# A feed-forward down-projection whose last product of each block is made in two halves

## The chip, the cores and the metric

The kernel runs on one core of a Trainium2 chip. The metric is the time of one execution on the device in microseconds (us). The core has four engines that matter here: TensorE (PE in the profile; PEld are its weight loads), VectorE (DVE), ScalarE (ACT) and GpSimd (POOL). DMA queues bring the weights from the chip's memory; SP issues these DMAs.

## The reference

One decoder layer: 256 tokens of width 1024 in float32. A normalised input goes through one combined projection into two token mixers, a recurrent one (RWKV-7) and a block-sparse attention (MoBA). Both are projected back, gated, merged, sent through an output projection and added to the input. The second half is the feed-forward part, which is where the change lies:

```python
def conv_ffn(h, w_up, conv_w, conv_b, w_down):
    u = h @ w_up
    a, b = u[..., :D_FF], u[..., D_FF:]
    a = lax.conv_general_dilated(
        a, conv_w.reshape(CONV_WIDTH, 1, D_FF), window_strides=(1,),
        padding=[(CONV_WIDTH - 1, 0)], dimension_numbers=('NWC', 'WIO', 'NWC'),
        feature_group_count=D_FF) + conv_b
    return (jax.nn.gelu(a, approximate=False) * b) @ w_down
```

with D_FF = 2816; the layer's output is x + conv_ffn(h2), where h2 is the normalised x.

## The kernel before

**Products in halves.** TensorE is used with operands rounded to a shorter float format (float32r). To keep the accuracy, each operand is split into a high and a low part (ACT rounds the high part, DVE makes the low part as the remainder), and a product of two matrices is made as three: high x high, low x high and high x low. All three accumulate into the same PSUM tile. So whatever is computed by `pe.matmul` in the kernel comes in groups of three lines: 346, 348, 351 in the helper `wst` (weights are the stationary operand and 256 tokens the moving one), 367, 368, 371 in `xst` (tokens stationary, up to 512 weight columns moving), and 1464, 1466, 1468 in the down-projection.

**Weights.** A queue lists all weight blocks of the layer in the order of their use. A block has 128 partitions by 1024 floats, 512 KB. A DMA on SP's queue brings it into a `raw` buffer (4 of them), `split_hi` (line 299, nearly always ACT) writes `whi` (4 buffers) and `split_lo` (line 310, DVE) writes `wlo` (3 buffers). The function `weights()` hands out the next pair and at once issues the split of a later block and the load of another one behind that. A `whi` or `wlo` buffer is written again only once the products that read it are done, so the splits wait on products.

**The feed-forward part.** The 2816 hidden columns are worked off in 11 blocks of 256, j = 0 to 10. In each block:

- `up()` makes 256 columns of the first half of the up-projection: four weight blocks, 48 products of 256 columns (8 pieces of the contraction x 2 groups of 128 hidden columns x 3). The stationary operand is `whi` or `wlo`, the moving one is `hx`, the normalised tokens in their high and low parts. DVE and ACT scale it, convolve it and apply GELU.
- `up(atp)` makes the matching 256 columns of the second half, 48 products again. DVE multiplies the two, and the result is split into high and low (`hb`).
- `down(j - 1)` makes the down-projection of the block before. It runs one block late, so that `hb` is ready when TensorE gets there.

`down` takes two weight blocks (i = 0, 1), one for each 128 hidden columns. For each it goes over four quarters of the output, f = 0 to 3: token half t by output half hf. Each quarter is an accumulator `fin[f]` of 128 tokens by 512 columns, a whole PSUM bank, held through all 11 blocks. Each quarter gets three products of 512 columns with `hb` as the stationary operand and `whi` or `wlo` as the moving one. That makes 2 x 4 x 3 = 24 products of 512 in a row. The next instruction on TensorE is the next block's `up()` with its 48 + 48 products of 256 columns.

`down` is called for j = 0 to 9. The block j = 10 is written out behind the loop (lines 1522 to 1524): its first three quarters in 18 products of 512 columns, the fourth in 12 products of 256 columns, six of them into a free accumulator, so that the last results leave in smaller pieces. For j = 9 the row of 24 is therefore followed by another 18 of 512.

**Order.** The feed-forward part is written out in program order; no planner chooses it. Each engine works off its own instructions in that order, and semaphores connect them. Every `pe.matmul` becomes two instructions of TensorE, a weight load for the stationary operand and the product itself.

Of the kernel before, what the change touches and what calls it, by code (L numbers as in the profile page):

```python
# [37 lines left out]
def body(tc, x, positions, norm1_g, w_in, rwkv_mu, w_decay_up, decay_bias, w_aaa_up,  # L38
# [3 lines left out]
    act, dve, pool, pe = nc.scalar, nc.vector, nc.gpsimd, nc.tensor  # L42
    ctx = ExitStack()
    with ctx:
# [12 lines left out]
        def b4(name, shape=(128, 4, 256), dt=F32):  # L57
            return sb.tile(list(shape), dt, name=name, tag="b4", bufs=NB4)
# [14 lines left out]
        def chp(name="ch"):  # L73
            return ps.tile([128, 512], F32, name=name, tag="ch", bufs=3)

        def atp(name="at"):
            return ps.tile([128, 512], F32, name=name, tag="at", bufs=2)
# [243 lines left out]
        def weights(n=1):  # L321

            w = ready.pop(0)
            taken[0] += 1
            for _ in range(n):
                with tc.issue_after(fence[0]) if taken[0] < 6 else nullcontext():
                    split_lo()
                    split_hi()
            return w
# [1093 lines left out]
        for i, (c0, c1) in enumerate(zip(WCUT, WCUT[1:])):  # L1423
            cs = slice(c0, c1)
# [31 lines left out]
        def down(j, hb):  # L1456
            for i in range(2):
                wh, wl = weights()
                st = j == 0 and i == 0
                for f in range(4):  # L1460
                    t, hf = divmod(f, 2)
                    ts = slice(t * 128, t * 128 + 128)
                    cs = slice(hf * 512, hf * 512 + 512)
                    pe.matmul(fin[f], hb[:, 0, i, ts], wh[:, 0, cs], start=st, stop=False,  # L1464
                              skip_group_check=f == 3)
                    pe.matmul(fin[f], hb[:, 1, i, ts], wh[:, 0, cs], start=False, stop=False,  # L1466
                              skip_group_check=f == 3)
                    pe.matmul(fin[f], hb[:, 0, i, ts], wl[:, 0, cs], start=False, stop=False,  # L1468
                              skip_group_check=f == 3)

        prev = []
        for j in range(11):
            hb = b4("hb", (128, 2, 2, 256), F32R)
            if j == 0:
# [3 lines left out]
                fin = [chp("f0"), chp("f1"), chp("f2"), atp("f3")]  # L1478
# [24 lines left out]
            if len(prev) == 2:  # L1503
                down(*prev.pop(0))
        of = out.rearrange("b s d -> (b s) d")
        j, hb = prev.pop(0)
# [6 lines left out]
        for f, is_ in ((0, (0,)), (1, (0,)), (0, (1,)), (2, (0,)), (1, (1,)), (2, (1,)), (3, (0, 1)), (4, (0, 1))):  # L1513
            t, hf = divmod(min(f, 3), 2)
            ts = slice(t * 128, t * 128 + 128)
            c0, n = ((0, 512), (0, 256), (256, 256))[max(f - 2, 0)]
            fs = last if f == 4 else fin[f][:, c0:c0 + n]
            cs = slice(hf * 512 + c0, hf * 512 + c0 + n)
            kw = dict(skip_group_check=True) if f == 3 else {}
            for i in is_:  # L1520
                wh, wl = ws[i]
# [32 lines left out]
```

## Time and profile before

| what | value |
|---|---|
| three timed runs | 402.75, 402.79, 403.62 us, median 402.79 |
| the profiled execution's own time | 402.01 us |
| its span, from the first instruction to the last | 400.2 us |
| PE busy | 394.3 us, 99% of the span |
| PEld busy | 365.9 us, 91% |
| DVE busy | 301.9 us, 75% |
| ACT busy | 237.3 us, 59% |
| the ten calls of `down` in the profile | 238.2 to 391.4 us, 80 products on each of the three lines |

A product's duration in the profile isn't what it costs. Products are pipelined and overlap: one with 256 columns is shown with about 277 ns, one with 512 with about 390 ns. What counts for the time is the distance between the starts of two neighbouring products. The timeline of PE shows these starts with two decimals of a microsecond, so distances are best read over many products at once.

Two more conventions of the rows: `f<-whi,hb` names the tile that is written and the tiles that are read (f is any of the four accumulators `fin`), and in a row of the groups the number behind the bar is the busy time, the mean duration in ns, and then the idle time of the engine just before these instructions. In a table by stretches each row has the stretch, its length, then PE, PEld, DVE, ACT and POOL with busy time and count, the granted clock of TensorE, the share of the DMA engines and GB/s.

### The profile page before, as it was taken

To read this page: it belongs to the slowest core of one execution; us is meant where nothing else is said; L and a number is where in the kernel's file an instruction comes from. 1 tells how busy PE (TensorE), PEld (TensorE's weight loads), DVE (VectorE), ACT (ScalarE), POOL (GpSimd) and SP (SyncE) were. 2 spreads that over 40 slices of the span, in tenths; PEclk is the share of its full clock that TensorE was granted. 3 is DMA by queue.
4 is the path that set the end of the run, shared out by engine and by line. 5 is a ranking of instruction groups with operands and counts; after the bars stand their busy time and mean duration, and the time that the engine had idled before them with its cause. 6 is when DMAs were issued, how large, how long until landed. Compare 5 with 4: busy or idle time off the path is not lost.

```text
span 400.2 us, 9024 instructions
## 1 busy us (share of the span) xinstructions
PE 394.3 (99%) x3633; PEld 365.9 (91%) x3633; DVE 301.9 (75%) x508; ACT 237.3 (59%) x411; POOL 49.5 (12%) x87
## 2 busy tenths in 40 slices
PE   8999999999999999999999999999999999999996
PEld 6899999898999989999888999999999999999995
DVE  4989989899868989688875885765757667576583
ACT  5899477494747686635554874554545546455350
POOL 8888000010600021120000000000000000000000
PEclk9999999999999999999999999999999999999999
DMA  8943397554694333555661765666665565665612
GB/s 255 323 147 86 86 305 219 139 153 124 145 292 128 108 98 128 201 162 185 199 195 56 261 206 184 196 189 195 191 208 186 185 208 168 204 211 163 208 52 105
DMA packets 60589, 70.58 MB, mean 176 GB/s; under 512 B 7377, under 2 KB 51287, under 8 KB 60548
## 3 DMA queue, kind: packets, MB, share of 16 engines
q1 hardware_dynamic: 58116, 69.17, 56.1%
q10 hardware_dynamic: 1632, 0.59, 0.6%
q8 instruction: 28, 0.46, 0.5%
q0 software_dynamic: 800, 0.26, 0.4%
q14 instruction: 13, 0.11, 0.1%
HBM read 68.56 MB, written 1.44 MB: 175 GB/s over the span
## 4 chain that ended last, share of the span: by engine, by line
PE 85%; POOL 4%; DMA 4%; DVE 3%; ACT 1%; issue 1%; SPq 0%; POOLq 0%
PE acc L346 11%; PE acc L351 11%; PE acc L348 11%; PE at L351 5%; PE at L346 5%; PE at L348 5%; PE f L1468 5%; PE f L1466 5%; PE f L1464 5%; PE acc L367 4%; PE acc L371 4%; PE acc L368 4%; DMA posi<-in_positions_dram 2%; PE acc L1322 2%; PE pq L1323 1%; DMA p<-in_aaa_bias_dram 1%
## 5 line engine op out<-in xcount | busy, mean ns | idle before, releaser
L299 ACT CAST whi<-raw 128x1024 fp32r<-128x1024 f32 (+1 forms) x122 | 124.5, 1025 | 111.3 <-PE acc L348 44.0
L310 DVE TENSOR_TENSOR wlo<-raw,whi 128x1024 fp32r<-128x1024 f32 (+1 forms) x122 | 144.6, 1188 | 37.7 <-PE f L1468 14.4
L346 PE MATMUL acc<-hx,whi 128*128 128x256 f32 x400 | 99.4, 284 | 0.0
L348 PE MATMUL acc<-hx,whi 128*128 128x256 f32 x400 | 97.1, 279 | 0.0
L346 PEld LDWEIGHTS acc<-hx,whi 128*128 128x128 f32 x400 | 75.4, 188 | 2.4 <-issue 0.8
L348 PEld LDWEIGHTS acc<-hx,whi 128*128 128x128 f32 x400 | 75.4, 188 | 0.4
L351 PE MATMUL acc<-hx,wlo 128*128 128x256 f32 x400 | 62.3, 278 | 0.2 <-DVE rs L1440 0.2
L351 PEld LDWEIGHTS acc<-hx,wlo 128*128 128x128 f32 x400 | 53.2, 188 | 0.4 <-DVE wlo L310 0.4
L346 PE MATMUL at<-hx,whi 128*128 128x256 f32 x176 | 42.4, 278 | 0.0
L348 PE MATMUL at<-hx,whi 128*128 128x256 f32 x176 | 42.3, 277 | 0.0
L348 PEld LDWEIGHTS at<-hx,whi 128*128 128x128 f32 x176 | 33.1, 188 | 0.0
L346 PEld LDWEIGHTS at<-hx,whi 128*128 128x128 f32 x176 | 33.1, 188 | 0.0
L1468 PE MATMUL f<-wlo,hb 128*128 128x512 f32 x80 | 31.6, 395 | 0.0
L1466 PE MATMUL f<-whi,hb 128*128 128x512 f32 x80 | 31.4, 393 | 0.0
L1464 PE MATMUL f<-whi,hb 128*128 128x512 f32 x80 | 31.2, 390 | 0.0
L351 PE MATMUL at<-hx,wlo 128*128 128x256 f32 x176 | 27.3, 277 | 0.0
L351 PEld LDWEIGHTS at<-hx,wlo 128*128 128x128 f32 x176 | 23.3, 188 | 0.0
L1466 PEld LDWEIGHTS f<-whi,hb 128*128 128x128 f32 x80 | 15.0, 188 | 3.1
L1468 PEld LDWEIGHTS f<-wlo,hb 128*128 128x128 f32 x80 | 15.1, 189 | 3.0
L1464 PEld LDWEIGHTS f<-whi,hb 128*128 128x128 f32 x80 | 15.0, 188 | 2.9
L1482 DVE TENSOR_TENSOR an<-acc,rsb 128x512 f32<-128x512 f32 x11 | 7.6, 692 | 13.1 <-PE acc L351 12.9
L1499 DVE TENSOR_TENSOR cv<-cv,at 128x256 f32<-128x256 f32 x22 | 8.3, 417 | 10.2 <-PE at L351 9.9
(359 smaller groups left out, 696.2 us busy)
## 6 DMA issues: line engine op xcount, KB each, us to landing
raw<-in_w_ffn_up_dram SPq DMA_DIRECT2D x44, 512.0 KB, 3.6
raw<-in_w_in_dram SPq DMA_DIRECT2D x33, 512.0 KB, 4.7
raw<-in_w_ffn_down_dram SPq DMA_DIRECT2D x22, 512.0 KB, 3.4
raw<-in_w_out_dram SPq DMA_DIRECT2D x8, 512.0 KB, 4.2
raw<-in_w_in_dram SPq DMA_DIRECT2D x8, 272.0 KB, 2.9
early<-in_w_in_dram SPq DMA_DIRECT2D x2, 1024.0 KB, 8.1
raw<-in_w_branch_b_dram SPq DMA_DIRECT2D x4, 512.0 KB, 3.5
raw<-in_w_branch_a_dram SPq DMA_DIRECT2D x4, 512.0 KB, 3.4
```

The source lines that it names most:

```text
L299: act.copy(wide(hi, k, c), spread(raw, k, c))
L310: eng.tensor_tensor(wide(lo, k, c), spread(raw, k, c), wide(hi, k, c).bitcast(F32), op=OP.subtract)
L346: pe.matmul(om, wh[:, k, ms], xh[:, k0 + k], start=k0 + k + m == 0, stop=False, skip_group_check=True)
L348: pe.matmul(om, wh[:, k, ms], xl[:, k0 + k], start=False, stop=False, skip_group_check=True)
L351: pe.matmul(om, wl[:, k, ms], xh[:, k0 + k], start=False, stop=k0 + k == nk - 1 and m == n - 1, skip_group_check=True)
L367: pe.matmul(ps_[t], xh[:, K, ts], wh[:, k], start=K == 0, stop=False)
L368: pe.matmul(ps_[t], xl[:, K, ts], wh[:, k], start=False, stop=False)
L371: pe.matmul(ps_[t], xh[:, K, ts], wl[:, k], start=False, stop=K == nk - 1)
L1464: pe.matmul(fin[f], hb[:, 0, i, ts], wh[:, 0, cs], start=st, stop=False, skip_group_check=f == 3)
L1466: pe.matmul(fin[f], hb[:, 1, i, ts], wh[:, 0, cs], start=False, stop=False, skip_group_check=f == 3)
L1468: pe.matmul(fin[f], hb[:, 0, i, ts], wl[:, 0, cs], start=False, stop=False, skip_group_check=f == 3)
L1499: dve.tensor_tensor(cv, cv, pb[:, m], op=OP.mult)
```

## The change

The third product of the last quarter (f = 3) of the second weight block (i = 1) is no longer one product of 512 columns. It is made as two of 256 columns, on the left and the right half of the same accumulator, with the same stationary operand. All other products of `down` stay as they are, and so does the order. A call of `down` has then 23 products of 512 columns in a row and two of 256 behind them.

```diff
                     pe.matmul(fin[f], hb[:, 1, i, ts], wh[:, 0, cs], start=False, stop=False,
                               skip_group_check=f == 3)
-                    pe.matmul(fin[f], hb[:, 0, i, ts], wl[:, 0, cs], start=False, stop=False,
-                              skip_group_check=f == 3)
+
+                    for c in ((0, 512),) if f < 3 or i == 0 else ((0, 256), (256, 512)):
+                        pe.matmul(fin[f][:, c[0]:c[1]], hb[:, 0, i, ts],
+                                  wl[:, 0, hf * 512 + c[0]:hf * 512 + c[1]], start=False, stop=False,
+                                  skip_group_check=f == 3)
```

## The prediction

> **What bounds the kernel now.** The page comes first: span, engine totals and the chain that ended last.
>
> ```profile
> span 400.2 us, 9024 instructions
> PE 394.3 (99%) x3633; PEld 365.9 (91%) x3633; DVE 301.9 (75%) x508; ACT 237.3 (59%) x411; POOL 49.5 (12%) x87
> ...
> PE 85%; POOL 4%; DMA 4%; DVE 3%; ACT 1%; issue 1%; SPq 0%; POOLq 0%
> ```
>
> The chain runs on TensorE (PE) for 85% of the span, and there is one weight load for each product: 3633 of both. The second view is the table by stretches, cut at the feed-forward part: one down-projection, the two up-projections of the next block, one down-projection, and then all nine later blocks together.
>
> ```profile
> 238.20:243.80 5.60, 5.60 (x26) 4.56 (x25) 3.78 (x6) 2.55 (x5) 0.00 (x0) 1.00 0.62 199
> 243.80:249.30 5.50, 5.50 (x50) 5.49 (x49) 2.45 (x2) 2.32 (x3) 0.00 (x0) 1.00 0.56 183
> 249.30:254.70 5.40, 5.40 (x50) 5.40 (x49) 4.54 (x7) 3.83 (x7) 0.00 (x0) 1.00 0.65 193
> 254.70:260.20 5.50, 5.50 (x26) 4.53 (x25) 3.79 (x6) 2.56 (x5) 0.00 (x0) 1.00 0.67 205
> 238.30:385.80 147.50, 147.50 (x1081) 138.61 (x1079) 97.02 (x135) 78.14 (x109) 0.00 (x0) 1.00 0.60 190
> ```
>
> The second column is PE: busy in every microsecond from 238.3 to 385.8, at a granted clock of 1.00. DVE is busy for 97.0 and ACT for 78.1 of those 147.5 us, so neither can be what ends last here. Nothing in this part waits; its time is the number of products times the distance from one start to the next (the pitch). The third view, the groups by line and shape in the same stretch, has no idle time before any of the three lines that the change touches:
>
> ```profile
> L1468 PE MATMUL f<-wlo,hb 128*128 128x512 f32 x72 | 28.4, 395 | 0.0
> L1466 PE MATMUL f<-whi,hb 128*128 128x512 f32 x72 | 28.3, 393 | 0.0
> L1464 PE MATMUL f<-whi,hb 128*128 128x512 f32 x72 | 28.1, 390 | 0.0
> ```
>
> The 390 to 395 ns in these rows are durations of overlapping products. What a product costs is the pitch, which has to come from the timeline of PE. Here is one down-projection with its neighbours: first its first product, then its last two, then the first products of the next up-projection, then the starts of the up-projection after it and of the next down-projection.
>
> ```profile
> 271.11 0.39 PE L1464 MATMUL f<-whi,hb 128*128 128x512 f32 x1
> ...
> 276.14 0.39 PE L1466 MATMUL f<-whi,hb 128*128 128x512 f32 x1
> 276.37 0.39 PE L1468 MATMUL f<-wlo,hb 128*128 128x512 f32 x1
> 276.61 0.28 PE L346 MATMUL acc<-hx,whi 128*128 128x256 f32 x1
> 276.72 0.28 PE L348 MATMUL acc<-hx,whi 128*128 128x256 f32 x1
> 276.84 0.28 PE L346 MATMUL acc<-hx,whi 128*128 128x256 f32 x1
> 276.96 0.28 PE L348 MATMUL acc<-hx,whi 128*128 128x256 f32 x1
> 277.08 0.28 PE L346 MATMUL acc<-hx,whi 128*128 128x256 f32 x1
> 277.20 0.28 PE L348 MATMUL acc<-hx,whi 128*128 128x256 f32 x1
> ...
> 282.07 0.28 PE L346 MATMUL at<-hx,whi 128*128 128x256 f32 x1
> 287.51 0.39 PE L1464 MATMUL f<-whi,hb 128*128 128x512 f32 x1
> ```
>
> Three pitches follow. (a) 24 products of 512 columns take 276.61 - 271.11 = 5.50 us: 0.229 each. (b) The 48 products of 256 in the second up-projection take 287.51 - 282.07 = 5.44 us: 0.1133 each. (c) The 48 of the first take 282.07 - 276.61 = 5.46, and the excess lies at their beginning: the first five take 277.20 - 276.61 = 0.59 where five at (b) take 0.567. So a change from down to up costs about 0.025 us. The whole of what follows agrees with these three:
>
> ```profile
> 243.81 0.28 PE L346 MATMUL acc<-hx,whi 128*128 128x256 f32 x1
> ...
> 385.91 0.39 PE L1464 MATMUL f<-whi,hb 128*128 128x512 f32 x1
> ```
>
> Between these rows lie nine blocks of up-projections, 9 x 96 products, and eight down-projections, 8 x 24. 864 x 0.1133 + 192 x 0.229 + 9 x 0.025 = 142.1 us, and 385.91 - 243.81 is 142.10. So all nine changes from down to up end at the pace (b).
>
> There is a second pace, and the argument on the risk rests on it. Just before, the same up-projection code ran slower, and so did the first down-projection:
>
> ```profile
> 222.54 0.41 PE L1445 MATMUL prs<-ident,rx 128*128 128x128 f32 x2
> 222.79 0.24 PE L1446 MATMUL prs<-ident,p 88*128 88x88 f32 x1
> 222.82 0.36 PE L346 MATMUL at<-hx,whi 128*128 128x256 f32 x1
> ...
> 232.56 0.28 PE L346 MATMUL at<-hx,whi 128*128 128x256 f32 x1
> ...
> 238.21 0.40 PE L1464 MATMUL f<-whi,hb 128*128 128x512 f32 x1
> ```
>
> 48 products from 232.56 to 238.21 take 5.65 us: 0.1177 each, 4.4 ns over (b). 24 products from 238.21 to 243.81 take 5.60: 0.2333, 4.2 ns over (a). The slow pace sets in after three small transposes cut into the stream, and it lasts, with the clock at 1.00 and PE without idle, until the change from down to up at 243.81, after which (b) holds. The trace doesn't say what the pace is. It says that an interruption can set it, that it then stays, and that a change of shape can end it.
>
> **The change part by part.** It touches the third product (line 1468) of the fourth quarter (f = 3) of the second weight block (i = 1), in each of the ten calls of `down` (j = 0 to 9; the block j = 10 is written out behind the loop and stays). It removes 10 products of 512 columns and adds 20 of 256, with 10 more weight loads since each product has its own. Order, operands, waits and DMAs stay.
>
> **The pair itself.** The nearest row is in the tail, where products with the same kinds of operands, on the same accumulator, go from 512 to 256 columns:
>
> ```profile
> 395.29 0.40 PE L1524 MATMUL f<-wlo,hb 128*128 128x512 f32 x1
> 395.53 0.28 PE L1522 MATMUL f<-whi,hb 128*128 128x256 f32 x1
> 395.64 0.28 PE L1523 MATMUL f<-whi,hb 128*128 128x256 f32 x1
> ...
> 396.77 0.28 PE L1524 MATMUL acc<-wlo,hb 128*128 128x256 f32 x1
> ```
>
> The eleven pitches from 395.53 to 396.77 make 1.24 us, 0.1127 each at this rounding: pace (b), and from the first one on. So a pair costs 2 x 0.1133 = 0.2266 against 0.229: -2.4 ns, ten times -0.024 us. The upper bound is a pair at the slow pace, 2 x 0.1177 = 0.2354: +6.4 ns, ten times +0.064. The extra weight load lies under the product before it, as all others here; a pitch of 0.1133 with a load for each product is what the up-projections do throughout. If that cover were gone, the price is the slow pace below.
>
> The Trainium skill's page "TensorE: Matmul & The Clock Gate", section "Back-to-back issue gap", speaks against the edit: columns / 2.4 GHz plus a fixed 2.5 ns a product, so two halves cost one fixed part more. By it the sum would be 10 x (2 x 109.2 - 215.8) ns = +0.025 us (an estimate). This trace differs on both sizes (0.1133 and 0.229), and here two halves come out cheaper than one whole.
>
> **The slow start of the next up-projection** (0.025 us, nine of them; the tenth pair stands ahead of the tail's products of 512). If the change of width brings it, the pair swallows part or all of it: at best 9 x 0.025 = -0.22 us. If it comes from the change of operands (at that point hx becomes the moving operand and whi the stationary one), it stays. The tail changes width without operands and has no slow start, so I take it to stay: 0. The lower bound is -0.22, the upper 0.
>
> **Releases.** ACT and DVE wait for these products before they write the next weight halves:
>
> ```profile
> ACT whi L299 <- PE f L1466: 26.6, 18, 1.7
> DVE wlo L310 <- PE f L1468: 14.4, 10, 1.6
> ```
>
> The release of wlo now hangs on the second half of the pair, which ends within 0.01 us of where the whole one ended. Those waits are slack of engines that aren't the bound (PE never idles), so: 0. Were that cover gone, ten releases 0.01 us late would be 0.1 us.
>
> **Sum.** -0.02 us, with bounds of -0.24 and +0.06. The profiled execution took 402.01 us: the span of 400.2 and 1.8 around it; it becomes 401.99. The three timed runs (402.75, 402.79, 403.62) lie 0.7 to 1.6 above it, and their median, against which the result is told, becomes 402.77: **402.8**. About 0.2%, 0.8 us, is what a measurement of this kernel can tell from no change, so this is no change.
>
> **Rivals.**
>
> *The slow pace takes hold (slower).* After the pair, the up-projection starts at another phase of loads and products and stays at the slow pace, as it did from 222.8 on. The price of a block is 96 x 4.4 + 24 x 4.2 = 523 ns; nine blocks from 244 to the tail make 4.7, and the tail's 30 products about 0.1: **407.6**. It decides as soon as two blocks stay slow (1.05 us). For it: the slow pace outlived a change of shape at 238.21, and all blocks repeat alike, so what happens in one likely happens in nine. Against it: all nine changes from down to up in this trace, and the tail's change of width, ended in the fast pace. The Trainium skill's page "TensorE: Matmul & The Clock Gate", section "LDWEIGHTS (loading the stationary operand)", has columns / 1.2 GHz, so 107 ns for a load of 128 (an estimate): under a product of 256 there are 6 ns to spare, under one of 512 over 100. This leaves room for a late load; that 256 columns in a row need not bring one, the tail shows.
>
> *It takes hold in some blocks only.* One block in the slow pace is +0.5, four are +2.1: **403.3 to 404.9**.
>
> *The row itself gets faster (faster).* The 512-column products of the output projection give a better pitch than (a):
>
> ```profile
> 195.12 0.39 PE L367 MATMUL acc<-whi,mh 128*128 128x512 f32 x1
> ...
> 196.48 0.39 PE L367 MATMUL acc<-whi,mh 128*128 128x512 f32 x1
> ```
>
> Six products (367, 368, 367, 368 and two of 371) in 1.36 us: 0.2267. If the pair resets whatever makes (a) slower, 23 x 10 products gain 2.3 ns each, 0.53 us; with the slow starts gone too it is 0.53 + 0.22 + 0.02 = 0.77: **402.0**. A gain of that size also comes if the timed runs, 0.8 us above the profiled one, hold one or two slow blocks that it lacks and the pair ends them: 402.79 - 2 x 0.52 = **401.7**. Against both: the operands of the row are unchanged, and nothing before the pair can know of it except through the block before.
>
> *The change doesn't do what it says*, because a half goes without its own weight load, the stationary operand being the same. The page's 3633 loads for 3633 products speak against that, and it would be 402.8 all the same.
>
> **How the numbers follow.** Forecast, with the saved load: 0.62 (its own range 402.3 to 403.3, the spread of the runs shown around it). Slow pace everywhere: 0.17. In some blocks: 0.07, of which 0.05 are over 0.8 us. Faster row or slow blocks ended: 0.14, of which I put 0.12 over 0.8 us, since the two can add up. So faster 0.12, slower 0.17 + 0.05 = 0.22, same 0.66. The range reaches down to the faster rival and up past four slow blocks, 401.7 to 405.0, and leaves out the slow pace everywhere and 0.02 at the low end.
>
> **What would show it.** Right: the timeline has the pair at 0.113 each, the next up-projection with its five slow products, and 48 products in 5.44 to 5.46 us in every later block; weight loads and products at 3643 each. Wrong: up-projections of 5.65 us with no idle on PE (the slow pace), rows of 23 in clearly less than 5.27 us (23 x 0.229), or the five slow starts gone. A wait on PE ahead of line 346 would mean that I mis-judged the releases.

## The result and the profile after

The changed kernel takes 407.41 us (median of 5 runs, 406.26 to 409.21) where the kernel before takes 403.34 on the same chip (5 runs, 402.75 to 403.62). The ratio is 1.0111 with a 95% interval of 1.008 to 1.0142: slower, by 3.2 to 5.7 us. The forecast was 402.8 and no change. The time lies outside the range and close to the price of the rival "the slow pace takes hold" (407.6).

The page of the changed kernel's profiled execution (406.26 us by its own time):

```profile
span 404.5 us, 9044 instructions
PE 398.7 (99%) x3643; PEld 369.9 (91%) x3643; DVE 301.8 (75%) x508; ACT 237.3 (59%) x411; POOL 48.5 (12%) x87
```

The change does what it says: 3643 products and as many loads, ten more than before. PE is busy for 4.4 us longer; the work of DVE and ACT is the same. Where PE's time comes from stands in the table by stretches, the two up-projections behind the first changed down-projection, and the whole feed-forward part:

```profile
243.40:249.05 5.65, 5.65 (x51) 5.65 (x49) 2.45 (x2) 2.30 (x3) 0.00 (x0) 1.00 0.58 183
249.05:254.70 5.65, 5.65 (x50) 5.65 (x49) 4.54 (x7) 3.86 (x7) 0.00 (x0) 1.00 0.57 181
223.00:395.50 172.50, 172.50 (x1241) 162.41 (x1241) 113.18 (x161) 91.28 (x130) 0.00 (x0) 1.00 0.58 182
```

PE is never idle and its granted clock is 1.00 throughout, yet each up-projection takes 5.65 us where it took 5.46 and 5.44. The timeline of PE shows the first row, the pair of the second row and what stands around it, and the first product of the tail:

```profile
237.79 0.40 PE L1464 MATMUL f<-whi,hb 128*128 128x512 f32 x1
...
254.70 0.40 PE L1464 MATMUL f<-whi,hb 128*128 128x512 f32 x1
...
260.07 0.40 PE L1470 MATMUL f<-wlo,hb 128*128 128x256 f32 x2
260.30 0.28 PE L346 MATMUL acc<-hx,whi 128*128 128x256 f32 x1
...
265.95 0.28 PE L346 MATMUL at<-hx,whi 128*128 128x256 f32 x1
...
271.61 0.40 PE L1464 MATMUL f<-whi,hb 128*128 128x512 f32 x1
...
395.56 0.40 PE L1525 MATMUL f<-whi,hb 128*128 128x512 f32 x1
```

The 23 products take 260.07 - 254.70 = 5.37 us, 0.2335 each; the pair takes 0.23; the two up-projections take 5.65 and 5.66, 0.1178 a product. That is the slow pace. In the kernel before, the same block begins and the tail begins here:

```profile
254.71 0.39 PE L1464 MATMUL f<-whi,hb 128*128 128x512 f32 x1
...
391.41 0.39 PE L1522 MATMUL f<-whi,hb 128*128 128x512 f32 x1
```

A block costs 271.61 - 254.70 = 16.91 us, where it cost 271.11 - 254.71 = 16.40 before: +0.51. From the first down-projection to the tail (395.56 here, 391.41 before) it is 157.77 us against 153.20, so 4.57 more. Eight blocks at 0.507 make 4.06 of it, the first block, whose row was slow before too, 0.40, and the tenth row 0.11. By kind of product, 3.6 us of it lie in the up-projections of the nine blocks and 1.0 in the rows of the down-projection. The two spans differ by 4.3, because this execution reached its first down-projection 0.42 us sooner (237.79 against 238.21), which lies ahead of the first changed product, and spent 0.15 more from the start of the tail on.

### The profile page after: what moved, and what is told of

Read it like the earlier page. It is cut to its first block, busy times and chain, and to the rows that moved or that the text cites. A ratio compares the mean times of both kernels' runs of the same rounds, so it can differ in the third digit from the quotient of the medians.

```text
span 404.5 us, 9044 instructions
## 1 busy us (share of the span) xinstructions
PE 398.7 (99%) x3643; PEld 369.9 (91%) x3643; DVE 301.8 (75%) x508; ACT 237.3 (59%) x411; POOL 48.5 (12%) x87
## 4 chain that ended last, share of the span: by engine, by line
PE 90%; DVE 4%; ACT 2%; DMA 1%; issue 1%; POOL 1%; SPq 0%; DVEq 0%; ACTq 0%
PE acc L346 13%; PE acc L351 12%; PE acc L348 12%; PE at L351 5%; PE at L346 5%; PE at L348 5%; PE f L1464 5%; PE f L1470 5%; PE f L1466 5%; PE acc L367 4%; PE acc L371 4%; PE acc L368 4%; PE acc L1322 1%; PE pq L1323 1%; DMA raw<-in_w_in_dram 1%; PE pgr L773 1%
## 5 line engine op out<-in xcount | busy, mean ns | idle before, releaser
L346 PE MATMUL at<-hx,whi 128*128 128x256 f32 x176 | 43.6, 282 | 0.0
L348 PE MATMUL at<-hx,whi 128*128 128x256 f32 x176 | 43.5, 281 | 0.0
L1464 PE MATMUL f<-whi,hb 128*128 128x512 f32 x80 | 31.8, 398 | 0.0
L1466 PE MATMUL f<-whi,hb 128*128 128x512 f32 x80 | 31.8, 398 | 0.0
L1470 PE MATMUL f<-wlo,hb 128*128 128x512 f32 (+1 forms) x90 | 31.8, 371 | 0.0
L1470 PEld LDWEIGHTS f<-wlo,hb 128*128 128x128 f32 x90 | 17.1, 189 | 3.9
```

The costliest lines, as they stand in the source:

```text
L346: pe.matmul(om, wh[:, k, ms], xh[:, k0 + k], start=k0 + k + m == 0, stop=False, skip_group_check=True)
L348: pe.matmul(om, wh[:, k, ms], xl[:, k0 + k], start=False, stop=False, skip_group_check=True)
L1470: pe.matmul(fin[f][:, c[0]:c[1]], hb[:, 0, i, ts], wl[:, 0, hf * 512 + c[0]:hf * 512 + c[1]], start=False, stop=False, skip_group_check=f ...
```

## The experiments

The question was what makes a block slow: that the row is too short to end the slow pace (a length theory), or that the pair sets it (a pair theory). Neither held in the end, and a third was formed: the pace is decided anew at each change in the stream, by the place at which the row stands then (a phase theory). It covers most of what follows, but not all.

Times of single executions differ by up to 3 us for one kernel (the kernel before: 401.86 to 404.93 in 19 runs), so the verdicts go by the paces in the traces, and by times only where there are several. Each trace is one execution.

**The pair from the second block on.** The first row keeps its 24 products.

```diff
-                    for c in ((0, 512),) if f < 3 or i == 0 else ((0, 256), (256, 512)):
+                    for c in ((0, 512),) if f < 3 or i == 0 or j == 0 else ((0, 256), (256, 512)):
```

> The pair is made in the blocks j = 1 to 9 only; the first down-projection keeps its 24 products of 512 in a row. Length theory (the pair doesn't start the slow pace; it only makes the row too short to end it, and the fast pace stays once it is there): the first row ends the slow pace, all later blocks run at 0.1133 in spite of their pairs, and the time is that of the kernel before within 0.8 us, some 403. Pair theory (a pair right ahead of an up-projection sets the slow pace by itself): the first up-projection behind a pair is slow, eight blocks of 0.52 us and the tail make +4.2, some 407.5.

407.38 us, median of 4, against 402.66; ratio 1.0104 (1.0078 to 1.0129). The timeline from the first row that has a pair, one block behind the whole one:

```profile
256.09 0.39 PE L1464 MATMUL f<-whi,hb 128*128 128x512 f32 x1
...
261.35 0.40 PE L1470 MATMUL f<-wlo,hb 128*128 128x256 f32 x2
261.59 0.28 PE L346 MATMUL acc<-hx,whi 128*128 128x256 f32 x1
...
267.24 0.28 PE L346 MATMUL at<-hx,whi 128*128 128x256 f32 x1
```

The whole first row has ended the slow pace: the 23 products take 261.35 - 256.09 = 5.26 us, 0.229 each. Then comes the pair, and the up-projection behind it takes 267.24 - 261.59 = 5.65 us. So the pair not only fails to end the slow pace, it brings it into a fast stream. The length theory falls.

**23 in a row without a pair.** The 24th product of each row isn't made, so ten of the 22 products with the low part of the weights are missing in the last quarter.

```diff
-                    pe.matmul(fin[f], hb[:, 0, i, ts], wl[:, 0, cs], ...
+                    if f < 3 or i == 0:
+                        pe.matmul(fin[f], hb[:, 0, i, ts], wl[:, 0, cs], ...
```

> No pair; the 24th product of each row is left out (a tenth of what the last quarter's low part of the weights gives is missing), so 23 of 512 stand directly ahead of the up-projection. Length theory: 23 are as too few as with the pair behind them; up-projections at 5.65 us each, 10 x 0.23 less for the products, so 403.3 - 2.3 + 4.7 = some 405.7. Pair theory: as the kernel before, up-projections at 5.44 us, 403.3 - 2.3 = 401.0.

399.73 us in one run. 23 products directly ahead of the up-projection keep the fast pace in all blocks:

```profile
254.47 0.39 PE L1464 MATMUL f<-whi,hb 128*128 128x512 f32 x1
...
259.74 0.28 PE L346 MATMUL acc<-hx,whi 128*128 128x256 f32 x1
...
265.19 0.28 PE L346 MATMUL at<-hx,whi 128*128 128x256 f32 x1
...
270.63 0.39 PE L1464 MATMUL f<-whi,hb 128*128 128x512 f32 x1
```

5.27, 5.45 and 5.44 us. Directly ahead of an up-projection, 23 of 512 do no harm; it takes the pair between them.

**The pair at another place.** The third product of the first quarter instead of the last.

```diff
-... if f < 3 or i == 0 else ((0, 256), (256, 512)):
+... if f > 0 or i == 1 else ((0, 256), (256, 512)):
```

> The pair is made of the third product of the first quarter (i = 0, f = 0) instead of the last, so that 21 products of 512 stand behind it and the row ends in a 512 as before. Length theory: 21 in a row, or 23 in all, are too few, the slow pace stays in every block, +4.1, some 407.5. Pair theory (it has to stand ahead of the up-projection): as the kernel before, 403.3 within 0.8.

405.01 us in one run, halfway between the two expectations, and the trace says why. Fast and slow blocks take turns:

```profile
245.09 0.28 PE L346 MATMUL acc<-hx,whi 128*128 128x256 f32 x1
...
250.54 0.28 PE L346 MATMUL at<-hx,whi 128*128 128x256 f32 x1
...
261.48 0.28 PE L346 MATMUL acc<-hx,whi 128*128 128x256 f32 x1
...
267.14 0.28 PE L346 MATMUL at<-hx,whi 128*128 128x256 f32 x1
...
278.31 0.28 PE L346 MATMUL acc<-hx,whi 128*128 128x256 f32 x1
```

5.45 us behind the first row, 5.66 behind the second; the third is fast again, and so on to the end. Neither theory has room for that. The row behind a slow block starts slow (its first distance is 236 ns, where it is 228 behind a fast block), and its last distances are some 232, 226, 236 instead of 229, 232, 226: the rows come to their end in two different ways.

**28 in a row.** A fourth product, low times low, in the four quarters of i = 1.

```diff
+                    if i == 1:
+                        pe.matmul(fin[f], hb[:, 1, i, ts], wl[:, 0, cs], ...
```

> The kernel before with a fourth product (low times low) in the four quarters of i = 1, so that a row has 28 products of 512. Cost of the products 40 x 0.229 = 9.2 us, some 412.5. Length theory: in the first row, which starts slow, the pitch goes from 0.2333 to 0.229 at about the 24th product, with four or five fast products behind it in the same row. Rival (it is the change from 512 to 256 columns that ends the slow pace, however long the row): all 28 are slow and the pace ends at the first up-projection behind them.

414.33 us in one run, 1.8 above the sum in the expectation. In the first row all 28 products are slow, and the pace ends at the change to the up-projection, as the rival had it; a long row alone doesn't end it. But here too blocks take turns: slow up-projections behind every second row.

```profile
239.55 0.40 PE L1464 MATMUL f<-whi,hb 128*128 128x512 f32 x1
...
246.09 0.28 PE L346 MATMUL acc<-hx,whi 128*128 128x256 f32 x1
...
256.99 0.39 PE L1464 MATMUL f<-whi,hb 128*128 128x512 f32 x1
...
263.39 0.28 PE L346 MATMUL acc<-hx,whi 128*128 128x256 f32 x1
...
269.05 0.28 PE L346 MATMUL at<-hx,whi 128*128 128x256 f32 x1
```

28 products in 6.53 us (0.2333 each), then two up-projections in 10.90 (fast); 28 in 6.41 us (0.2289), then an up-projection of 5.66 (slow). There is no 256-column pair in this kernel's rows at all, so a pair can't be the only thing that brings the slow pace, and the pair theory falls too.

**What the starts in the trace show.** The trace has the starts to the ns, and the distances between them, read row by row, gave the next theory. A bar marks a change of width or operands, and dots stand for what goes on alike:

```
distances between starts, ns                             row of 512 | pair(s) | up-projection
before, 271.11     227 229 231 227 229 232 ... 225 229 231 | 119 115 118 123 119 113 112
changed, 254.70    236 233 234 233 234 233 ... 234 | 118 115 | 115 118 117 118 118 119
pair from 2nd      228 229 232 226 229 231 ... 232 226 229 | 120 118 | 115 118 118 117 119
23, no pair        228 229 232 225 230 231 ... 229 232 225 236 | 117 117 120 115 115 113
28                 227 230 231 226 230 231 ... 228 232 226 | 119 116 119 118 117
```

A fast row isn't even: its distances repeat in threes, some 226, 229 and 232 ns, whatever the lines of the products are. A slow row is even at 233 to 234, but for its first products. So at the end of a fast row the stream stands on the first, second or third of the three, and that goes by the length of the row: 24 ends on the third, 23 on the second, 28 on the first. Behind a fast row, as in the second block of the first experiment, the pair makes the stream change its width at the second place, with the same operands. (The rows of the changed kernel itself are slow to their end and have no such places.)

**Two tests of it.** The last three, or the last two products of the row are made as pairs, from the second block on; the first row stays whole.

```diff
+                    for n, (a, w) in enumerate(((0, wh), (1, wh), (0, wl))):
+                        for c0, c1 in ((0, 256), (256, 512)) if j > 0 and i == 1 and f == 3 else ((0, 512),):
+                            pe.matmul(fin[f][:, c0:c1], hb[:, a, i, ts], w[:, 0, hf * 512 + c0:hf * 512 + c1], ...
```

with `and n > 0` for two.

> From the second block on, the last three products of the row are made as pairs, so 21 of 512 stand ahead of six of 256; the first row keeps its 24. Phase theory (in a fast row the pitches repeat in threes, about 226, 229, 232 ns; a row that ends on the third of them goes over to 256 columns in the fast pace, as the tail of the kernel before did after 42, and a row that ends on the first or the second goes over slowly, as 23 did): 21 ends on the third, all pairs and up-projections run at 0.1133, and the time is the one before less 27 x 2.4 ns and at best the slow starts, 402.4 to 402.7. Pair theory (any pair ahead of an up-projection sets the slow pace): some 407.

> The same with the last two products as pairs: 22 of 512 ahead of four of 256. Phase theory: 22 ends on the first of the three, slow pace in the blocks behind it, some 407. Pair theory: also some 407. A theory by which only an odd number of pairs does harm: 402.6.

For the pairs behind a fast row the phase theory was right both times, for the up-projections wrong both times. Three pairs behind 21:

```profile
260.87 0.39 PE L1466 MATMUL f<-whi,hb 128*128 128x256 f32 x2
...
261.55 0.28 PE L346 MATMUL acc<-hx,whi 128*128 128x256 f32 x1
...
267.21 0.28 PE L346 MATMUL at<-hx,whi 128*128 128x256 f32 x1
...
277.76 0.28 PE L1466 MATMUL f<-whi,hb 128*128 128x256 f32 x1
...
278.47 0.28 PE L346 MATMUL acc<-hx,whi 128*128 128x256 f32 x1
...
283.92 0.28 PE L346 MATMUL at<-hx,whi 128*128 128x256 f32 x1
```

The six products at 260.87 take 0.68 us (0.1133: fast), and the up-projection behind them 5.66 (slow). In the next block, whose row is slow, the six take 0.707 (0.1178: slow), and the up-projection 5.45 (fast). So here the change of operands from down to up, at an unchanged width, turns the pace over. The median of 7 runs is 405.30, against 403.26; ratio 1.0051 (1.0024 to 1.0078), since every second block is slow. Two pairs behind 22:

```profile
257.29 0.39 PE L1466 MATMUL f<-whi,hb 128*128 128x512 f32 x1
...
262.79 0.29 PE L346 MATMUL acc<-hx,whi 128*128 128x256 f32 x1
...
268.25 0.28 PE L346 MATMUL at<-hx,whi 128*128 128x256 f32 x1
...
273.69 0.39 PE L1466 MATMUL f<-whi,hb 128*128 128x512 f32 x1
```

The four products of 256 are slow (118, 118, 118 and 117 ns in the trace), the up-projection behind them is fast (5.46 and 5.44 us), and it is so in every block: 273.69 - 257.29 = 16.40 us, as before the change. Here two products are split instead of one, and in this trace the split costs nothing in the blocks. The single run took 404.70, but its first down-projection began only at 240.79, 2.6 us later than in the kernel before, and from there to the tail it is as long as there (153.2 us). The delay lies far ahead of the change: 1.6 us of it arise between 36 and 46 us, where the granted clock was 0.93 and 0.90 (30 to 40 and 40 to 50 us) in this execution and 1.00 in that of the kernel before.

**All 24 as pairs**, from the second block on (the condition above is `j > 0` alone): no change of width, only of operands.

> The first row keeps its 24 products of 512; from the second block on all 24 products are made as pairs, 48 of 256, so the width never changes again until the tail. Phase theory: the fast pace, once there, isn't touched; each later row takes 48 x 0.1133 = 5.44 instead of 5.49 us and the slow starts are gone, 9 x (0.055 + 0.025) = -0.7 us, some 402.0. Rival (the change of operands between down and up alone can set the slow pace): slow blocks, some 407 to 408.

```profile
256.28 0.28 PE L1466 MATMUL f<-whi,hb 128*128 128x256 f32 x1
...
261.72 0.28 PE L346 MATMUL acc<-hx,whi 128*128 128x256 f32 x1
...
267.38 0.28 PE L346 MATMUL at<-hx,whi 128*128 128x256 f32 x1
...
273.03 0.28 PE L1466 MATMUL f<-whi,hb 128*128 128x256 f32 x1
...
278.69 0.28 PE L346 MATMUL acc<-hx,whi 128*128 128x256 f32 x1
...
284.14 0.28 PE L346 MATMUL at<-hx,whi 128*128 128x256 f32 x1
```

A fast down-projection of 5.44, then 5.66, 5.65 and 5.66, then 5.45: fast and slow turn over at each change from down to up, and the change from up to down keeps the pace. 404.97 us, median of 12, ratio 1.0042 (1.0024 to 1.0061). The rival had the mechanism, and less than half of its price (1.7 us, where it had put some 4 to 5), since only every second block is slow.

**The last four products as pairs** (20 of 512, ending on the second of the three as 23 does), to see whether that place or the shortness of a single pair makes the up-projection slow.

```diff
-... if j > 0 and i == 1 and f == 3 and n > 0 else ((0, 512),):
+... if j > 0 and i == 1 and 3 * f + n > 7 else ((0, 512),):
```

> From the second block on, the last four products of the row as pairs: 20 of 512 ahead of eight of 256; the first row keeps its 24. Phase theory: 20 ends on the second of the three, as 23 does, so the pairs run slow (0.118). What the up-projection behind them does tells two versions apart. If the pace turns over at the change of operands once the pairs have settled (as behind four slow and six fast ones), it is fast, and the blocks cost as much as before, some 403. If ending on the second of the three makes the up-projection slow too, as behind the one pair of the changed kernel: 5.65 us, some 407.

404.93 us in one run. The blocks don't all go alike, because the first row began otherwise than in the other kernels: its distances are 235, 231, 237, 232, 231, then 226, 229, 232 and so on to 227, and the up-projection behind it is slow (5.65 us from 244.12). Its code up to there is that of the kernel before, whose first row is slow to its end. What differs is the pace ahead of the interruption at 222.9 us: 117 to 119 ns a product here, 112 to 115 in the kernel before. So the same code doesn't take the same way in each execution. Behind that, three ways occur. Where the row is fast and ends on the second place, the eight pairs' products are slow, and the up-projection is slow too:

```profile
288.75 0.39 PE L1466 MATMUL f<-whi,hb 128*128 128x512 f32 x1
...
293.33 0.28 PE L1466 MATMUL f<-wlo,hb 128*128 128x256 f32 x1
...
294.27 0.28 PE L346 MATMUL acc<-hx,whi 128*128 128x256 f32 x1
...
299.92 0.28 PE L346 MATMUL at<-hx,whi 128*128 128x256 f32 x1
```

20 products in 4.58 us (0.229), eight in 0.94 (0.1175), 48 in 5.65. So behind a fast row it is the place, not that there is one pair only: 23 and 20 give slow blocks, 22 doesn't. Where the row was slow throughout, the pairs were slow and the up-projection fast (from 277.86, 5.45 us). Where the row turned fast in its course and ended on the third place, the pairs were fast and the up-projection slow (from 260.93, 5.66 us), as with three pairs behind 21. Both kinds of slow pairs have the same pace, and yet the up-projection goes two ways behind them. Only the last of the eight distances differs, 115 ns behind the fast row and 117 to 118 behind the slow one. So the pace alone doesn't say what comes next.

**The interruption ahead of it all.** The slow pace of the kernel before begins behind three small transposes in the first block. Three kernels leave all products of the down-projection alone and touch only these transposes: their order, and one or two more of the token scale, written to an unused part of the same tile.

```diff
             pe.transpose(p[:, S:S + 88], p2, ident[:88, :88])
+            for _ in range(1):        # or range(2)
+                pe.transpose(p[:, 384:512], rx[:, 1], ident)
             act.copy(rsb, p[:, 0:S])
```

> The kernel before, with the transpose of the convolution's parameters issued ahead of the two of the token scale, so that the stream of the first block is cut into at two places instead of one; no product of the down-projection is changed. If the slow pace of 223 to 244 us is set by the form of that interruption, the first blocks may run fast: 129 x 4.4 + 24 x 4.2 ns = -0.7 us, some 402.0. If any interruption there sets it: 402.7 as before.

> The kernel before with one more small transpose (of the token scale, into an unused part of the same tile) behind the three that cut into the first block's up-projection; it costs 0.11 us at most and changes only the place at which the stream of 256 columns goes on. If the pace behind an interruption is a matter of that place, it may come out fast from 224 us on: -0.67 + 0.1 us against the kernel before, and the first up-projections at 5.44 instead of 5.65 us. If any interruption here sets the slow pace: 5.65 us as before.

> The same with two more small transposes instead of one, 0.22 us at most: another place. Expected as for one more; if the places come in threes, one of the three numbers (none, one, two) gives the fast pace.

The other order changes nothing: 403.09 us, and the up-projections from 227.99 on take 5.65 us as before. One more transpose:

```profile
227.16 0.28 PE L346 MATMUL acc<-hx,whi 128*128 128x256 f32 x1
...
232.60 0.28 PE L346 MATMUL at<-hx,whi 128*128 128x256 f32 x1
...
238.04 0.39 PE L1466 MATMUL f<-whi,hb 128*128 128x512 f32 x1
...
243.53 0.28 PE L346 MATMUL acc<-hx,whi 128*128 128x256 f32 x1
```

5.44, 5.44 and 24 products in 5.49: fast from the interruption on, and to the end of the kernel. 401.77 us beside 402.77. Two more:

```profile
239.02 0.40 PE L1466 MATMUL f<-whi,hb 128*128 128x512 f32 x1
...
244.53 0.28 PE L346 MATMUL acc<-hx,whi 128*128 128x256 f32 x1
...
250.19 0.28 PE L346 MATMUL at<-hx,whi 128*128 128x256 f32 x1
...
255.84 0.40 PE L1466 MATMUL f<-whi,hb 128*128 128x512 f32 x1
```

406.59 us beside 402.77. The rows have all their 24 products, no pair is anywhere, and yet every up-projection to the end takes 5.65 us. This is another slow place than in the kernel before: here the row leaves the slow pace after five products (235, 232, 236, 232, 232, then 226, 229, 231 and so on), comes to its end on the first of the three instead of the third, and falls back. Two small transposes, 0.19 us together and 15 us ahead of the first down-projection, do as much harm as the change did: from the interruption to the last 12 products it takes 176.87 us, where it took 172.98 in the kernel before and 172.40 with one transpose more.

**The kernel with one more transpose, timed.**

> The kernel with one more transpose, timed. If the place at which the stream goes on behind the interruption is the same in every execution, the fast pace from 224 us on is worth 0.7 us less 0.05 us for the transpose in each of them: a ratio of 0.9984 against the kernel before. If it falls now here, now there (an execution that lands as the kernel with two more transposes did is some 4 us slower), the runs spread over several us and the median is no lower than before.

402.02 us, median of 12 (401.09 to 402.93), against 403.06, median of 17 (401.93 to 404.25); ratio 0.9978 (0.9962 to 0.9993). It is faster than the kernel before, by 0.3 to 1.5 us. The traces explain 0.6 of that: the first block's slow pace had cost 0.67 us, and the transpose costs 0.08. The profiled executions of the two runs came to the interruption at different paces (117 to 119 ns and 113 to 114) and both left it at the fast one.

**What the runs show together.** What comes out at a change can be put in a table. All cases are read from the distances in the traces. The numbers are the products of 512 in the row, and a row that begins slow and turns fast in its course is left out. "At once" means that no pairs stand between the row and the up-projection.

| the row of 512 ends | then products of 256 with the same operands | then, or at once, the up-projection |
|---|---|---|
| fast, on the third place | fast (21; 42 in the tail) | slow behind pairs (21); fast at once (24) |
| fast, on the first place | slow (22) | fast behind pairs (22); slow at once (28; 21 behind an early pair) |
| fast, on the second place | slow (20, 23; 41 in a tail) | slow behind pairs (20, 23); fast at once (23) |
| slow to its end | slow behind 20 and 21; slow, then near 114, with one pair behind 23 | fast behind three or four pairs; slow behind one pair; fast at once (23, 24, 28) |

The tails bear the first half of the table out. In all 14 traces the tail goes from a row of 512 that is fast at its end to products of 256 with the same operands. Where the row ends on the third place (six traces), they take 113 ns; where it ends on the first or second (eight traces), 118.

Shown is that the pace changes at such places of the stream, and that behind a fast row it goes by the place where the row ends. Between them it mostly stays; the exception are rows that begin slow and turn fast behind some five products, every row with two more transposes and every second one with 28.

The changed kernel itself belongs in the last line of the table: its rows are slow to their end. That its pair is what makes its blocks slow is shown, by the first experiment, where a fast row of 23 with the pair behind it begins the slow pace, and by the second, where 23 without the pair keep the fast one. Why one pair behind 23 slow products leaves the up-projection slow, while three behind 21 and four behind 20 leave it fast, stays open: no run varied the number of pairs and the length of a slow row separately.

What in TensorE the three places are, and why the slow pace costs 4.4 ns a product at either width, no run shows. A weight load that comes late by a few ns would fit the products of 256 columns, but not those of 512, where the load has twice the time and the loss is the same. The traces show no late load either: at both paces and both widths a load is shown to begin 3.0 to 3.5 ns on average behind the start of a product, and to last 188 ns at the fast pace and 189 to 190 at the slow one.

## Why the prediction was wrong

**What bounds the kernel: right.** PE is never idle in the feed-forward part of either kernel, and the time is the number of products times their pitch. The two paces and their prices were right: a slow block was put at +0.523 us and measured at +0.51. That the slow kernel, put at 407.6, came out at 407.41 is closer than the working deserves: it had 4.8 us on a base of 402.77, and the measurement has 4.1 between the medians (3.2 to 5.7 by the ratio's interval) on a base of 403.34.

**"The pair itself": inside its bounds, but from the wrong row.** The pair was put at 0.2266 us with an upper bound of 0.2354, and took 0.233 (118 and 115 ns). Against the whole product's 0.229 that is +4 ns instead of -2.4, some 0.04 us in ten pairs. The tail was taken as the nearest row for what a change of width does, "from the first one on" at the fast pace. The tail's change stands behind a fast row of 42 products, the pair behind 23, and the tests with 20, 21, 22 and 23 show that behind a fast row the length decides the pace of what follows. The same operands and the same accumulator weren't enough to make the rows alike.

**"The slow start of the next up-projection ... I take it to stay: 0": the step that failed.** It allowed between -0.22 and 0 us for what happens at the change from down to up. The true term is +4.6 in the traces: at that place the pace of the next 96 products is decided (+3.6 in all), and the next row begins at the pace that they have (+1.0). The sum had no term for this, because the pace behind the change was taken to be fast whatever stood ahead of it. The five slow products at the start of each up-projection were read as a cost of 0.025 us. In the light of the experiments they may be the sign that the pace is settled anew at that place each time; no run tests that reading.

**The rival's chance (0.17) was too low, for one reason.** Against it stood "all nine changes from down to up in this trace, and the tail's change of width". These looked like ten trials. They are rows of 24 nine times, the first at the slow pace (0.2333) and eight alike at 0.229, and the tail's 42 is a multiple of three as well. The trace of before couldn't show another length. What spoke for the rival, that one block's outcome is likely all blocks' outcome, was right for this change: all nine are slow.

**"It takes hold in some blocks only"** didn't happen with this change, but it is what the early pair, three pairs and 48 halves do: every second block is at the slow pace, at 404.97 and 405.30 us in the two that were run several times.

**"The row itself gets faster"** didn't happen either: the fast row of 23 in the first experiment takes 5.26 us, 0.229 a product.

**The releases: right.** From 223 to 396 us PE waits for nothing in either kernel, before line 346 or elsewhere.

**The rule of the page.** The Trainium skill's page "TensorE: Matmul & The Clock Gate", section "Back-to-back issue gap", has one gap for each width, which it calls that of an isolated product; by it the change was put at +0.025 us (an estimate). The feed-forward part of these traces has two paces at each width at a granted clock of 1.00, 0.1133 and 0.1178 us for 256 columns, 0.229 and 0.2335 for 512, and the difference between them, not the fixed part, made the result.

## What to carry to other kernels

Where TensorE never waits, look at the pitch of its products over long stretches, not at their durations: if the same code runs at two paces in one trace, a small change of shape or order can move everything behind it from one to the other, and the price is the difference times all products up to the next change. A row that repeats nine times is one trial, not nine, and a neighbouring row is evidence only if the number of products ahead of it agrees too. Before a variant is thrown away for such a loss, it is worth trying the neighbours in count: from the second block on, two pairs behind 22 cost nothing in the blocks of their trace, where one pair behind 23 cost 4.7 us in four runs. Such a find has to be timed in many executions, since the same code can set out in another way in some of them.

## What the runs showed of the hardware

- One pace change costs 4.4 ns on every product: 5.65 us against 5.44 for 48 products of 256 columns, with the clock granted at 1.00 and no idle time in either.
- In a fast row of the down-projection the distances repeat in threes (226, 229, 232 ns). The lines of the products do so too, but with four products a quarter, in 16 of the 28 of a row, the threes of the distances stay, so they aren't those of the lines.
- One transpose more moved the time from the interruption to the last 12 products by -0.6 us, two more by +3.9 us (172.40 and 176.87 us against 172.98, one trace each).
- The same code can run at either pace in different executions. The first 127 products from 20.3 us on, ahead of everything that any of these kernels changes, were slow in four of the 14 traces and fast in ten; between the first of the traces compared here (slow) and that of the changed kernel (fast) this is 0.57 us.
- Executions of one kernel on one chip differ by up to 3 us. Part of it goes with the granted clock: of 36 runs of the kernel before, the six with a mean clock of 0.996 took 404.0 to 404.9 us, the 30 with 0.999 or 1.000 took 401.9 to 404.2. Part may be paces like the one above. Only profiled executions show those, so how much of the spread they make stays open.
